# A four-mixer scan block on one core: a head's token-major operands moved to the partitions of its feature-major ones

## The chip, the cores and the metric

The kernel runs on one core of one Trainium2 chip. A core has TensorE (PE: matrix products, with PEld for the loading of its stationary operand), VectorE (DVE), ScalarE (ACT), GpSimd (POOL) and SyncE (SP, which here issues nearly all DMAs). They run side by side, each through its own instructions in a fixed order, and wait for each other by semaphores. On-chip memory (SBUF, and PSUM for the results of TensorE) has 128 partitions; a product sums over the partitions of its two operands. The metric is the device time in microseconds.

## The reference

One layer of a trunk over 256 context and 2048 latent tokens of width 1024: a modulated RMS norm, one input projection whose columns feed four mixers, an output projection with a gated residual, a second norm, an MLP with squared ReLU, and a final norm. All in float32.

```python
def _gla_scan(q, k, v, log_a):
    ...
    att = jnp.einsum('bhnik,bhnjk->bhnij', q * jnp.exp(g - g_mid), k * jnp.exp(g_mid - g))
    att = jnp.where(_tri(0), att, 0.0)
    s_loc = jnp.einsum('bhnck,bhncv->bhnkv', k * jnp.exp(g_end[..., None, :] - g), v)
    def step(s, xs):
        s_l, ge = xs
        return jnp.exp(ge)[..., None] * s + s_l, s
    ...
    o = jnp.einsum('bhnik,bhnkv->bhniv', q * jnp.exp(g), s0) + jnp.einsum('bhnij,bhnjv->bhniv', att, v)
```

The other three mixers (mLSTM, RWKV-7 and Gated DeltaNet) have the same form with more terms: four heads each, chunks of 64 tokens, and an output that is a sum of two products, one with the state before the chunk (a sum over features) and one with the values of the chunk (a sum over its tokens). RWKV-7 and Gated DeltaNet also solve a triangular system in each chunk. Each mixer scans forward and backward, and the two results are added.

## The kernel before

The tokens are 36 chunks of 64. Six rounds (`ROUNDS`) of chunks pass through the input projection and leave every scan operand in device memory, in two layouts: feature-major (`x_fm`: 64 features of a head on 64 partitions, tokens along the row) and token-major (`x_tm`: 64 tokens on the partitions). `solve` inverts the triangular systems (`x_t`). Then come 72 calls of `group(d, c0)`, one for each direction and chunk, each for all four mixers and their 16 heads: two heads side by side in the row (`ft`), two on the two halves of the partitions (`par`). Eight of them (the context chunks) only update the state, 64 also give outputs. Where both directions have met, `finish` norms and gates the sum and stores it to `x_mix`. `tails` is the output projection and the MLP, on blocks of 512 tokens, with products of 128 x 128 by 512 columns.

`body` writes the program: the calls of `group` are strewn between the pieces of the rounds (32 calls), of the output gates (16) and of the first third of `tails` (24). A scheduler then settles the order on each engine from the dependences and its own estimate of durations, so that an edit in `group` moves instructions throughout. Tiles come from pools with a fixed number of buffers (two for most in the rounds and the tail, four in the gate phase); a transfer into a buffer waits until its earlier content was last read.

A call of `group` does the following. `ps_att` and `ps_ml` hold the products of the chunk's queries and keys; masks and decays make them the token-major operands. `ps_R` is the right side of the solve, made from the state; `ps_U` is the solution; `ps_S` the update of the state; the new state `St` is the old one by a decay (GpSimd) plus `ps_S` (VectorE). `ps_ym` and `ps_ylgr` are the outputs.

Before, a head's token-major operands lay on the other half of the partitions from its feature-major ones, in one tile: `L[:, par, x]` holds 64 rows of features and 64 rows of tokens, and `st[:, par, c]` the state beside the values of the tokens, which a DMA brings into the state's tile. One product over all 128 rows then gives the sum of both terms. The price is that each elementwise instruction that writes into `L` or `st` covers 64 partitions and stands twice, once for each `par`. `weave` orders the products of a bank and `mm` issues those without accumulation (both are one line for all callers, L228 and L239 in the profile; L184, L192 and L197 are the helpers `tt`, `stt` and `act`, and L200 is `dma`).

```python
        for par in R(2):
            q = other[par]
            self.tt(L[q, par, x], rk[q, x], m3[q, x], ALU.mult)
...
        self.weave(b, [(q, f2[ft], L[:, par, 1 + ft], st[:, par, cr(ft)]) for ft, par, p, q in fp]
                   + [(q, g2[ft], kw[p, ft], st[p, par, f2[ft]]) for ft, par, p, q in fp])
```

Of the kernel before, what the change touches and what calls it, by code (L numbers as in the profile page):

```python
# [96 lines left out]
def host_layout(I):  # L97
# [50 lines left out]
    A["nw"] = np.stack([f[k][0].reshape(2, 2, 64)[:, ::-1].transpose(0, 2, 1).reshape(128, 2)  # L148
# [5 lines left out]
    wo = f["w_out"][0].reshape(4, 2, 2, 64, 1024)[[0, 2, 3, 1]][:, :, ::-1].transpose(0, 2, 1, 3, 4).reshape(KT, 128, 1024)  # L154
# [21 lines left out]
class Kern:  # L176
# [133 lines left out]
    def scratch(self):  # L310
# [23 lines left out]
        self.td = 386, 1038  # L334
# [14 lines left out]
    def fill(self):  # L349
# [5 lines left out]
        for ft in range(2):  # L355
            c = 256 + 129 * ft
# [339 lines left out]
    def row_out(self, r, d, k0, t, p0):  # L696
# [3 lines left out]
        if k0 < 2:  # L700
            for par in range(2):
                self.dma(o[:, 1 - par, :, k0].rearrange("c f t -> f c t"), t[p0 + n * par:p0 + n * par + n, 0])
        else:
            self.dma(o[:, :, :, k0:k1].rearrange("c h f k t -> (h f) c (k t)"), t[p0:p0 + 2 * n].rearrange("p k t -> p (k t)"))
# [70 lines left out]
    def col_out(self, r, d, f0, srcs):  # L775
# [213 lines left out]
    def rw_group(self, r, ft, c0, c1, k, kk, wa, rr, v, gl):  # L989
# [68 lines left out]
        self.tm_out(r4(vt), X["tm"][c0:c1, :, :, 64 * ft:64 * ft + 64], nc_)  # L1058
# [21 lines left out]
    def ml_round(self, r):  # L1080
# [17 lines left out]
        yield from self.v_tiles(r, 18, 257)  # L1098
# [82 lines left out]
    def gl_round(self, r):  # L1181
# [54 lines left out]
        yield from self.v_tiles(r, 24, 128)  # L1236
# [95 lines left out]
    def solve_prep(self, d, c0, sN, A, B):  # L1332
# [18 lines left out]
        for par in R(2):  # L1351
            self.dma(gc[SL[par]].rearrange("p c k f -> p c (k f)"), X["tm"][c0:c0 + 2, :, 1 - par, self.td[d] + 320:self.td[d] + 326].rearrange("c t w -> t c w"))
# [23 lines left out]
    def solve_post(self, d, c0, sN, sD, sT, A, B):  # L1376
# [59 lines left out]
    def state_tile(self):  # L1436

        return self.wp.tile([128, 2, 514], F32, tag="St", name="St", bufs=4)
# [12 lines left out]
    def group(self, d, c0):  # L1451
# [5 lines left out]
        other = sl[::-1]  # L1457
# [12 lines left out]
        if hasq:  # L1470
            o = 13 if d else 6
            self.dma(kc, X["fm"][:, c0, o:o + 14])
        else:
            o = self.slot(d, 0)
            self.dma(ka[:, :4], X["fm"][:, c0, o:o + 4])
            self.dma(cfm[:, :2], X["fm"][:, c0, 13:15])
# [11 lines left out]
        tms, tmd = (tm[:, 0:320], tm[:, 320:652]) if d else (tm[:, 332:652], tm[:, 0:332])  # L1488
# [20 lines left out]
        for ft in R(2):  # L1509
            x, n = (2 * ft, 2) if hasq else (1 + ft, 1)  # L1510
            both = [(p, q, L[p, par]) for par, (p, q) in enumerate(zip(sl, other))]
            for p, q, l in both:
                self.mm(rk[q, x:x + n], ka[p, 3 * ft], l[:, x:x + n])
            if hasq:
                for p, q, l in both:
                    self.mm(ra[q, ft], ka[p, 1 + ft], l[:, 3 * ft])
                for p, q, l in both:
                    self.mm(pk[q, ft], cfm[p, ft], cfm[p, 2 + ft])
# [12 lines left out]
        if hasq:  # L1531
# [4 lines left out]
            for par in R(2):  # L1536
                q = other[par]
                self.tt(L[q, par, 6:8], ga[q], pk[q], ALU.mult)
        kw = self.wt("kw", [2, 64])
        self.tt(kw, cfm[:, 0:2], gr(2), ALU.mult)  # L1540
        if hasq:

            for par in R(2):
                p = sl[par]
                k2 = "p (k f) t -> p k f t"
                self.tt(L[p, par, 6:10].rearrange(k2, k=2), cfm[p, 2:6].rearrange(k2, k=2), rw[p, :, 3:5].rearrange("p f k t -> p k f t"),
                        ALU.mult)
# [5 lines left out]
        if hasq:  # L1553
# [26 lines left out]
            for par in R(2):  # L1580
                q = other[par]
                self.G.tensor_copy(L[q, par, 4:6], lS[q])
# [5 lines left out]
        fp = [(ft, par, sl[par], other[par]) for ft in R(2) for par in R(2)]  # L1588
# [339 lines left out]
```

## Time and profile before

| | us |
|---|---|
| median of 3 runs | 4356.84 (4348.51 to 4357.94) |
| the profiled execution | 4357.55 |
| its span | 4355.7 |
| busy in the span: TensorE | 3487.9 (80%) |
| VectorE | 2629.0 (60%) |
| GpSimd | 1557.1 (36%) |
| ScalarE | 1379.0 (32%) |

The span is what the profiler saw between the first and the last instruction. Busy time is the union of an engine's instructions. A row of the profile's groups names the line, the engine, the operation, the tile written and the tiles read, the tile shape of a product (rows*columns of the array) and partitions x elements; `ps_ylgr<-St,L 128*64 128x64` is a product into the bank `ps_ylgr` over 128 rows. Each of these products is two instructions on TensorE. A row of the waits names who waited for whom, the sum in us, how often, and the longest.

### The profile page before, as it was taken

The numbers are of one execution on the slowest core, as the hardware profiler recorded it, in microseconds if no ns is written. First come the engines' busy times: TensorE is split into PE (matmuls) and PEld (weight loads), VectorE is DVE, ScalarE is ACT, GpSimd is POOL, SyncE is SP. The second block draws the span as 40 slices with busy tenths as digits, with TensorE's granted clock in tenths as the row PEclk, the third lists the DMA queues.
The fourth block names the chain that finished last, engine by engine and source line by source line (L and its number), as shares of the span: only waits on it lengthen the run. The fifth ranks groups of instructions, "written<-read, shape, count | busy, mean of one in ns | idle before, by whom it ended". The sixth has DMA issues, their size and how long they took to land. (4 is left out here: it accounts for less than half of the span.)

```text
span 4355.7 us, 71098 instructions
## 1 busy us (share of the span) xinstructions
PE 3487.9 (80%) x26458; PEld 2787.2 (64%) x26458; DVE 2629.0 (60%) x5775; ACT 1379.0 (32%) x2482; POOL 1557.1 (36%) x1883
## 2 busy tenths in 40 slices
PE   6355876776686876655878699999999999999998
PEld 5234555555564655545766477777778878877886
DVE  7653765666386667636777466767774445445444
ACT  3224332432432233222323133222322332333322
POOL 3222635644154253512324333334542142224122
PEclk9667866886787687757778799999999999999999
DMA  6586466765766665577676544446453334332332
GB/s 213 123 181 153 101 161 153 162 127 141 149 161 124 166 155 129 129 176 169 176 196 181 160 129 145 137 151 167 134 155 100 96 100 131 97 97 87 116 94 86
DMA packets 718873, 610.62 MB, mean 140 GB/s; under 512 B 384784, under 2 KB 594784, under 8 KB 718528
## 3 DMA queue, kind: packets, MB, share of 16 engines
q1 hardware_dynamic: 718528, 606.08, 54.0%
q8 instruction: 209, 3.42, 0.4%
q14 instruction: 136, 1.11, 0.1%
HBM read 470.86 MB, written 135.03 MB: 139 GB/s over the span
## 5 line engine op out<-in xcount | busy, mean ns | idle before, releaser
L184 POOL TENSOR_TENSOR w_lo<-w_f,w_hi 128x1024 fp32r<-128x1024 f32 x213 | 518.3, 2433 | 1104.3 <-ACT w_hi L197 1074.0
L197 ACT ACTIVATE w_hi<-w_f 128x1024 fp32r<-128x1024 f32 (+1 forms) x427 | 448.3, 1050 | 935.4 <-PE ps_a L239 360.8
L239 PE MATMUL ps_a<-ah,w_hi 128*128 128x512 f32 x1024 | 406.4, 403 | 11.6 <-ACT ah L197 9.9
L239 PE MATMUL ps_f<-h2l,w_hi 128*128 128x512 f32 x1024 | 403.5, 394 | 9.3 <-DVE h2l L192 9.2
L239 PE MATMUL ps_f<-h2h,w_hi 128*128 128x512 f32 x1024 | 404.7, 396 | 4.0 <-ACT w_hi L197 2.7
L239 PE MATMUL ps_a<-al,w_hi 128*128 128x512 f32 x1024 | 405.0, 396 | 0.0
L239 PE MATMUL ps_f<-h2h,w_lo 128*128 128x512 f32 x1024 | 403.3, 394 | 1.0 <-DVE w_lo L184 1.0
L184 DVE TENSOR_TENSOR w_lo<-w_f,w_hi 128x1024 fp32r<-128x1024 f32 (+1 forms) x214 | 268.0, 1252 | 220.1 <-ACT w_hi L197 204.6
L239 PE MATMUL ps_a<-ah,w_lo 128*128 128x512 f32 x1024 | 397.7, 396 | 0.0
L239 PE MATMUL ps_z<-hh,w_hi 128*128 128x512 f32 (+3 forms) x760 | 308.7, 413 | 76.3 <-ACT hh L197 22.3
L192 DVE SCALAR_TENSOR_TENSOR x1T<-ps_a,modv,x1T 128x512 f32<-128x512 f32 x256 | 187.6, 747 | 227.7 <-PE ps_a L239 227.3
L239 PE MATMUL ps_z<-hh,w_lo 128*128 128x512 f32 (+3 forms) x760 | 307.1, 405 | 22.2 <-DVE w_lo L184 13.9
L239 PE MATMUL ps_z<-hl,w_hi 128*128 128x512 f32 (+3 forms) x760 | 304.6, 401 | 5.4 <-DVE hl L184 5.3
L184 DVE TENSOR_TENSOR relu<-relu 128x512 f32<-128x512 f32 x128 | 185.6, 1451 | 102.8 <-ACT relu L197 102.6
L211 PE MATMUL ps_z<-w_hi,hh 128*128 128x256 f32 x672 | 209.9, 314 | 38.0 <-ACT w_hi L197 17.2
L239 PEld LDWEIGHTS ps_a<-ah,w_hi 128*128 128x128 f32 x1024 | 192.0, 189 | 67.3 <-ACT ah L197 20.0
L239 PEld LDWEIGHTS ps_z<-hh,w_hi 128*128 128x128 f32 (+1 forms) x760 | 159.4, 211 | 116.8 <-ACT hh L197 24.6
L239 PEld LDWEIGHTS ps_f<-h2l,w_hi 128*128 128x128 f32 x1024 | 193.6, 189 | 51.7 <-DVE h2l L192 11.2
L239 PEld LDWEIGHTS ps_f<-h2h,w_hi 128*128 128x128 f32 x1024 | 194.0, 190 | 46.8 <-ACT w_hi L197 4.5
L239 PEld LDWEIGHTS ps_f<-h2h,w_lo 128*128 128x128 f32 x1024 | 193.8, 189 | 42.9 <-DVE w_lo L184 1.9
L239 PEld LDWEIGHTS ps_a<-ah,w_lo 128*128 128x128 f32 x1024 | 193.9, 189 | 42.6 <-issue 0.4
L239 PEld LDWEIGHTS ps_a<-al,w_hi 128*128 128x128 f32 x1024 | 193.8, 189 | 42.3 <-DVE al L184 0.4
(414 smaller groups left out, 8000.4 us busy)
## 6 DMA issues: line engine op xcount, KB each, us to landing
w_f<-w SPq DMA_DIRECT2D x256, 512.0 KB
w_f<-wg SPq DMA_DIRECT2D x90, 512.0 KB
kc<-x_fm SPq DMA_DIRECT2D x64, 448.0 KB
adaw<-ada SPq DMA_DIRECT2D x48, 512.0 KB
tm<-x_tm SPq DMA_DIRECT2D x144, 163.0 KB
rw<-x_rows SPq DMA_DIRECT2D x144, 160.0 KB
w_f<-wp SPq DMA_DIRECT2D x44, 512.0 KB
gat<-x_gat SPq DMA_DIRECT2D x64, 288.0 KB
```

What stands on the lines that cost most here:

```text
L184: return (e or self.V).tensor_tensor(out=o, in0=a, in1=b, op=op)
L192: return self.V.scalar_tensor_tensor(o, a, s, b, op0, op1)
L197: return self.S.activation(o, a, f, bias=bias, scale=scale)
L211: i = self.T.matmul(o, l, r, start=k == 0, stop=k == len(mms) - 1)
L239: return self.T.matmul(o, l, r, start=start, stop=stop)
```

## The change

Token-major operands move to the same half as the feature-major ones. So the tile `L` falls into three: `ff` (a part of the loaded tile `fm`), `Lq` and `Lt`; the values come into the tile `tm` and no longer into the state's; the state's tile is half as wide (514 columns for 2 x 514). An elementwise instruction covers 128 partitions and stands once. The two terms of a sum are now two products of 64 rows that accumulate in the bank. The second half of `ps_U` is no longer copied into the state's tile by VectorE (line 1602): ScalarE's copy `U` takes both halves. GpSimd's copy of `lS` into `L` (line 1582) is gone, since the product reads `lS`. The operands of one step lie together in `x_fm` and `x_tm`, so one DMA brings `fm` in place of three (`L` twice and `kc`), and the two for `tm` also bring what two for `St` did. Weights and norms are permuted on the host to suit, and the rows of `x_rows` are stored in one DMA for two.

```diff
-        return self.wp.tile([128, 2, 514], F32, tag="St", name="St", bufs=4)
+        return self.wp.tile([128, 514], F32, tag="St", name="St", bufs=4)
...
-        L = self.lt("L", [2, 10, 64])
-        lo, w = (0, 6) if hasq else (1, 2)
-        for par in R(2):
-            o = self.slot(d, 7 + lo)
-            self.dma(L[sl[par], par, lo:lo + w], X["fm"][sl[par], c0, o:o + w])
-        for par in R(2):
-            self.dma(st[other[par], par, 128:514], X["tm"][c0, :, 1 - par, 0:386])
-        kc = self.lt("kc", [14, 64])
-        ka, cfm = (kc[:, 7:14], kc[:, 0:7]) if d else (kc[:, 0:7], kc[:, 7:14])
+        fm = self.lt("fm", [20, 64])
+        ff, ka, cfm = (fm[:, x:x + n] for x, n in (((14, 6), (7, 7), (0, 7)) if d else ((0, 6), (6, 7), (13, 7))))
         if hasq:
-            o = 13 if d else 6
-            self.dma(kc, X["fm"][:, c0, o:o + 14])
+            o = 13 if d else 0
+            self.dma(fm, X["fm"][:, c0, o:o + 20])
...
-        tm = self.lt("tm", [652])
-        o = 718 if d else 386
-        self.by_half(tm, X["tm"][c0, :, :, o:o + 652])
+        tm = self.lt("tm", [1038])
+        o = 332 if d else 0
+        self.by_half(tm, X["tm"][c0, :, :, o:o + 1038])
...
-        for par in R(2):
-            q = other[par]
-            self.tt(L[q, par, x], rk[q, x], m3[q, x], ALU.mult)
+        self.tt(Lt[:, x], rk[:, x], m3[:, x], ALU.mult)
...
-            for par in R(2):
-                q = other[par]
-                self.G.tensor_copy(L[q, par, 4:6], lS[q])
...
-        self.weave(b, [(q, f2[ft], L[:, par, 1 + ft], st[:, par, cr(ft)]) for ft, par, p, q in fp]
-                   + [(q, g2[ft], kw[p, ft], st[p, par, f2[ft]]) for ft, par, p, q in fp])
+        self.weave(b, [(p, f2[ft], Lt[p, 1 + ft], vr(ft)[p]) for ft, p in fp]
+                   + [(p, f2[ft], ff[p, 1 + ft], st[p, cr(ft)]) for ft, p in fp]
+                   + [(p, g2[ft], kw[p, ft], st[p, f2[ft]]) for ft, p in fp])
...
-        U = self.wt("U", [128])
-        self.act(U, b.t[:, 0:128], AF.Copy)
-        for par in R(2):
-            q = other[par]
-            self.V.tensor_copy(st[q, par, 0:128], b.t[q, 128:256])
+        U = self.wt("U", [256])
+        self.act(U, b.t[:, 0:256], AF.Copy)
...
-        for par in R(2):
-            p = sl[par]
-            o = new[p, par, 0:256]
-            self.tt(o, o, b.t[p, 0:256], ALU.add)
...
+        self.tt(new[:, 0:256], new[:, 0:256], b.t[:, 0:256], ALU.add)
...
-                    first.append((q, y, L[:, par, x], st[:, par, c]))
+                    first.append((p, y, f[p], st[p, c]))
+                    then.append((p, y, t[p], v[p]))
                     if mm == "r":
-                        then.append((q, y, ara[q, ft], U[q, f2[ft]]))
-            self.weave(b, first + then)
+                        last.append((p, y, ara[p, ft], U[p, f2[ft]]))
+            self.weave(b, first + then + last)
```

What this does to the order of the instructions shows at three places, all in the part of the tail where the last steps still run. First TensorE, at the end of one step, between two products of the MLP (`ps_a`): what stood there before (`L` is the joined tile, `St` the joined state, `ara` an attention term; the shape is output rows x columns, x4 a repeat).

```order
L239 MATMUL ps_a<-ah,w_lo 128x512
L228 MATMUL ps_ylgr<-St,L 64x64
L228 MATMUL ps_S<-St,mke 32x65 x4
L228 MATMUL ps_S<-St,tm 32x64 x4
L228 MATMUL ps_S<-St,ke 64x64 x4
L228 MATMUL ps_S<-St,tm 64x64 x4
L228 MATMUL ps_S<-U,tm 64x64 x4
L228 MATMUL ps_ylgr<-St,L 64x64 x7
L228 MATMUL ps_ylgr<-U,ara 64x64 x4
L239 MATMUL ps_a<-ah,w_lo 128x512
```

And now, at the end of a step in the same part:

```order
L228 MATMUL ps_ylgr<-St,Lq 64x64 x2
L228 MATMUL ps_S<-tm,mke 32x65 x4
L228 MATMUL ps_S<-tm 32x64 x4
L228 MATMUL ps_S<-tm 64x64 x4
L228 MATMUL ps_S<-U,ke 64x64 x4
L228 MATMUL ps_S<-U,tm 64x64 x4
L228 MATMUL ps_ylgr<-St,Lq 64x64 x2
L228 MATMUL ps_ylgr<-St,fm 64x64 x4
L228 MATMUL ps_ylgr<-tm,glS_223 64x64 x4
L228 MATMUL ps_ylgr<-U,Lt 64x64 x4
L228 MATMUL ps_ylgr<-tm,Lt 64x64 x4
L228 MATMUL ps_ylgr<-U,ara 64x64 x4
```

`ps_S` has as many products as before; `ps_ylgr` has 28 for 16 in the whole step, and the change from products over 128 rows (`ps_ylgr<-St,L`) to products over 64 (`ps_ylgr<-U,ara`) within the bank is gone, as is that between `ps_S` and `ps_ylgr`.

Second VectorE, at the update of the state in that part; before (`fs` and `leg` are decays, `relu` and `al` belong to the MLP):

```order
L1602 COPY St<-ps_U 64x128 x2
L184 TENSOR_TENSOR relu<-relu 128x512
L184 TENSOR_TENSOR al<-relu,ah 128x512
L184 TENSOR_TENSOR St<-St,ps_S 64x256
L192 SCALAR_TENSOR_TENSOR St<-St,fs_82,ps_S 64x130
L192 SCALAR_TENSOR_TENSOR St<-St,leg,ps_S 64x128
L184 TENSOR_TENSOR St<-St,ps_S 64x256
L192 SCALAR_TENSOR_TENSOR St<-St,fs_82,ps_S 64x130
L192 SCALAR_TENSOR_TENSOR St<-St,leg,ps_S 64x128
L184 TENSOR_TENSOR L<-kc,rw 64x256 x2
```

And now:

```order
L184 TENSOR_TENSOR relu<-relu 128x512
L184 TENSOR_TENSOR al<-relu,ah 128x512 x2
L184 TENSOR_TENSOR St<-St,ps_S 128x256
L192 SCALAR_TENSOR_TENSOR St<-St,fs_82,ps_S 128x130
L192 SCALAR_TENSOR_TENSOR St<-St,leg,ps_S 128x128
L184 TENSOR_TENSOR yall<-ps_ylgr,gat 128x384
```

Ten instructions of the step became four; one of them, the product for `Lq`, stands ten rows behind the update now.

Third SyncE, the loads of one step among those of the MLP's weights (`w_f`); before (`t_26099` is the solved system's tile, `rw` the rows of gates, `gat` the gates and the other direction's output):

```order
L200 DMA L<-x_fm 64x384 x2
L200 DMA St<-x_tm 64x386 x2
L200 DMA rw<-x_rows_103 64x640 x2
L200 DMA w_f<-w 128x1024 x2
L200 DMA gat<-x_gat 64x1152 x2
L200 DMA w_f<-w 128x1024
L200 DMA x_mix<-sq 128x512
L200 DMA kc<-x_fm 128x896
L200 DMA t_26099<-x_t_132 128x2x128
L200 DMA w_f<-w 128x1024
L200 DMA tm<-x_tm 64x652
```

And now:

```order
L200 DMA fm<-x_fm 128x1280
L200 DMA tm<-x_tm 64x1038 x2
L200 DMA rw<-x_rows_103 64x640 x2
L200 DMA w_f<-w 128x1024
L200 DMA gat<-x_gat 64x1152 x2
L200 DMA w_f<-w 128x1024
L200 DMA x_mix<-sq 128x512
L200 DMA w_f<-w 128x1024
L200 DMA t_26538<-x_t_132 128x2x128
```

The loads of `kc` and of `tm`, which stood apart from those of `L` and `St`, now stand with `fm`, at the place where `L` stood.

More of the change, by code (lines that the diff above doesn't have):

```diff
@@ L699, in row_out @@
         o = self.X[f"rows{r}"][d]
[L700 to L704, printed above, removed]
+        self.dma(o[:, :, :, k0:k1].rearrange("c h f k t -> (h f) c (k t)"), t[p0:p0 + 2 * n].rearrange("p k t -> p (k t)"))
     def part(self, c):
@@ L1097, in ml_round @@
         yield
-        yield from self.v_tiles(r, 18, 257)
+        yield from self.v_tiles(r, 18, 589)
     def ml_scalars(self, r):
@@ L1235, in gl_round @@
             yield
-        yield from self.v_tiles(r, 24, 128)
+        yield from self.v_tiles(r, 24, 460)
     def common_pools(self):
@@ L1510, in group @@
             x, n = (2 * ft, 2) if hasq else (1 + ft, 1)
-            both = [(p, q, L[p, par]) for par, (p, q) in enumerate(zip(sl, other))]
-            for p, q, l in both:
-                self.mm(rk[q, x:x + n], ka[p, 3 * ft], l[:, x:x + n])
+            for p in sl:
+                self.mm(rk[p, x:x + n], ka[p, 3 * ft], ff[p, x:x + n])
             if hasq:
[L1515 to L1518, printed above, removed]
+                for p in sl:
+                    self.mm(ra[p, ft], ka[p, 1 + ft], ff[p, 3 * ft])
+                for p in sl:
+                    self.mm(pk[p, ft], cfm[p, ft], cfm[p, 2 + ft])
         m3 = self.rwm[d].rearrange("p (a t) -> p a t", t=64)
         x = slice(0, 4) if hasq else slice(1, 3)
-        for par in R(2):
-            q = other[par]
-            self.tt(L[q, par, x], rk[q, x], m3[q, x], ALU.mult)
+        self.tt(Lt[:, x], rk[:, x], m3[:, x], ALU.mult)
         if hasq:
@@ L1559, in group @@
             pm, ps = (b[:, x:x + 128].rearrange("p (f t) -> p f t", f=2) for x in (0, 128))
-            for par in R(2):
-                self.mm(pm[other[par]], cfm[sl[par], 6], cfm[sl[par], 4:6])
-            for par in R(2):
-                q = other[par]
-                self.tt(L[q, par, 8:10], md[q], pm[q], ALU.mult)
+            for p in sl:
+                self.mm(pm[p], cfm[p, 6], cfm[p, 4:6])
+            self.tt(Lt[:, 6:8], md, pm, ALU.mult)
             lS = self.glS[d][s % 2]
@@ L1587, in group @@
         b = chb("ps_R")
-        fp = [(ft, par, sl[par], other[par]) for ft in R(2) for par in R(2)]
-        self.weave(b, [(q, f2[ft], L[:, par, 1 + ft], st[:, par, cr(ft)]) for ft, par, p, q in fp]
-                   + [(q, g2[ft], kw[p, ft], st[p, par, f2[ft]]) for ft, par, p, q in fp])
+        fp = [(ft, p) for ft in R(2) for p in sl]
+        vr, vl, vm = (lambda ft, c=c: vs[:, c(ft).start - 128:c(ft).stop - 128] for c in (cr, cl, cm))
+        self.weave(b, [(p, f2[ft], Lt[p, 1 + ft], vr(ft)[p]) for ft, p in fp]
+                   + [(p, f2[ft], ff[p, 1 + ft], st[p, cr(ft)]) for ft, p in fp]
+                   + [(p, g2[ft], kw[p, ft], st[p, f2[ft]]) for ft, p in fp])
         rR, gR = self.wt("rR", [128]), self.wt("gR", [128])
@@ L1615, in group @@
         e = 0 if d else 63
[L1616 to L1628 removed]
+        for x, eg in ((0, rw[:, :, 3, e:e + 1]), (128, self.reg[:, d, :, c0:c0 + 1])):
+            y = slice(x, x + 128)
+            self.tt(v3(new[:, y]), v3(st[:, y]), eg.to_broadcast([128, 2, 64]), ALU.mult, e=self.G)
+        self.tt(new[:, 0:256], new[:, 0:256], b.t[:, 0:256], ALU.add)
+        for x, y, w, f in ((384, 256, 65, self.fs[d]), (256, 321, 64, self.leg[:, d])):
+            tw = lambda t: t.unsqueeze(1).to_broadcast([128, 2, w])
+            self.stt(new[:, x:x + 2 * w].rearrange(s3, f=2), tw(st[:, x:x + w]), f[:, c0:c0 + 1], tw(b.t[:, y:y + w]), ALU.mult, ALU.add)
         if not hasq:
@@ L1639, in group @@
             b = self.bank(self.qa, "yy", "ps_y" + ms, 1)
-            first, then = [], []
+            first, then, last = [], [], []
             for mi, mm in enumerate(ms):
                 w = 65 if mm == "m" else 64
-                for ft, par, p, q in fp:
+                for ft, p in fp:
                     y = slice(128 * mi + w * ft, 128 * mi + w * ft + w)
-                    x, c = {"m": (8 + ft, cm(ft)), "l": (4 + ft, cl(ft)), "g": (6 + ft, f2[ft]), "r": (3 * ft, cr(ft))}[mm]
-                    first.append((q, y, L[:, par, x], st[:, par, c]))
+                    f, c, t, v = {"m": (Lq[:, 2 + ft], cm(ft), Lt[:, 6 + ft], vm(ft)), "l": (ff[:, 4 + ft], cl(ft), lS[:, ft], vl(ft)),
+                                  "g": (Lq[:, ft], f2[ft], Lt[:, 4 + ft], U[:, g2[ft]]),
+                                  "r": (ff[:, 3 * ft], cr(ft), Lt[:, 3 * ft], vr(ft))}[mm]
+                    first.append((p, y, f[p], st[p, c]))
+                    then.append((p, y, t[p], v[p]))
                     if mm == "r":
-                        then.append((q, y, ara[q, ft], U[q, f2[ft]]))
-            self.weave(b, first + then)
+                        last.append((p, y, ara[p, ft], U[p, f2[ft]]))
+            self.weave(b, first + then + last)
             if ms == "m":
```

68 lines of the change are left out of this document (25 added, 43 removed).

## The prediction

> **What bounds the kernel now.** I read the busy times by stage first, then what TensorE waits for, then the products one by one, and last the groups of VectorE, GpSimd and SyncE. The stages are mine: the rounds and the gate phase (545 to 2440 us, where 48 of the 72 group steps end), the MLP tail while the other 24 still run (2440 to 3290), the tail alone. Columns: the stage, its length, then busy time with the number of instructions for TensorE, its weight loads, VectorE, ScalarE, GpSimd; granted TensorE clock, share of the DMA engines, GB/s.
>
> ```profile
> span 4355.7 us, 71098 instructions
> 545.00:2440.00 1895.00, 1343.47 (x14177) 1090.84 (x14176) 1218.34 (x3095) 619.70 (x1281) 747.73 (x1129) 0.73 0.65 154
> 2440.00:3290.00 850.00, 804.60 (x6218) 620.56 (x6219) 582.36 (x1318) 252.50 (x422) 342.34 (x337) 0.97 0.52 151
> 3290.00:4355.70 1065.70, 1027.35 (x4440) 829.28 (x4438) 495.18 (x530) 331.18 (x428) 285.02 (x136) 0.99 0.32 100
> ```
>
> The last stage holds no group step and stays as it is. In the one before it TensorE is busy 804.60 of 850 us: there the end moves with TensorE's own work. Before 2440 nothing is full: TensorE 71%, VectorE 64%. There the kernel lives on waits, and an instruction saved is worth what it shortens of one. These are TensorE's waits that the change touches (total, times, longest), first six before 2440, then two after:
>
> ```profile
> PE ps_R L228 <- DVE L L184: 40.0, 11, 11.9
> PE ps_att L239 <- DMA L<-x_fm: 18.5, 10, 5.1
> PE ps_S L228 <- DVE St L1602: 18.1, 11, 3.8
> PE ps_R L228 <- DVE St L192: 12.9, 5, 4.3
> PE ps_ym L228 <- DVE L L184: 11.7, 3, 6.9
> PE ps_ml L239 <- DVE L L184: 6.9, 11, 2.3
> ...
> PE ps_R L228 <- DVE L L184: 6.8, 2, 5.8
> PE ps_ym L228 <- DVE L L184: 3.0, 3, 2.3
> ```
>
> All the waits ahead of 2440 except the one on a DMA are for half-height VectorE work: 89.6 us in 41 waits, of 552 us that TensorE is idle there.
>
> **TensorE: more products, fewer changes of tile shape.** Counted in the code, a step with outputs has 20 products more (ps_R 8 to 12, ps_ym 4 to 8, ps_ylgr 16 to 28), one without has 4 more: 24 x 20 = 480 in the tail, 40 x 20 + 8 x 4 = 832 before it. Their price stands in one stretch of the tail; first column the start:
>
> ```profile
> 2810.35 0.45 PE L228 MATMUL ps_S<-St,ke 64*64 64x64 f32 x8
> 2810.63 0.40 PE L228 MATMUL ps_S<-St,tm 64*64 64x64 f32 x8
> 2810.86 0.40 PE L228 MATMUL ps_S<-U,tm 64*64 64x64 f32 x8
> 2811.20 0.92 PE L228 MATMUL ps_ylgr<-St,L 128*64 128x64 f32 x24
> 2812.04 0.45 PE L228 MATMUL ps_ylgr<-U,ara 64*64 64x64 f32 x8
> 2812.42 0.50 PE L239 MATMUL ps_a<-ah,w_hi 128*128 128x512 f32 x1
> ```
>
> A product of 64 columns is two instructions (12 products stand as x24). From start to start, 24 instructions of shape 128*64 take 0.84 us, 24 of shape 64*64 (ps_S) 0.85, eight of 64*64 0.38. So the 64-row product costs no less than the 128-row one: (0.84 - 0.38) / 16 = 0.029 us an instruction, 0.0575 a product, and each run of one shape carries 0.38 - 8 x 0.029 = 0.15 us beside. In the order of the instructions I counted the places where the tile shape changes: 492 before and 378 now in the tail, 1012 and 852 ahead of it. Tail: 480 x 0.0575 = 27.6 us more, 114 x 0.15 = 17.1 less, **+10.5**, with nothing to hide it on an engine 95% busy. Of it, 5 waits on L (9.8 us) shrink by about 0.8 us each, -4: **+6.5**.
>
> Ahead of the tail: 47.8 - 24 = 23.8 us at full clock, 32.6 at the granted 0.73. It ranges from nothing (all of it in the 552 idle us) to +32.6; since a group's products come in bursts that others wait for, I take half: **+16**.
>
> The Trainium skill speaks against the change here: "TensorEngine Tiling (Array Packing)", Restrictions and Gotchas, says that different row tiles cannot write one PSUM bank at the same time. The ps_S rows are two row tiles in one bank and run no slower than ps_ylgr's column tiles (0.85 against 0.84), so the trace doesn't bear it out; it is the last rival below.
>
> **VectorE and ScalarE: half as many half-height instructions.** The rows: instruction, partitions x elements, count; busy, mean ns; idle before.
>
> ```profile
> L184 DVE TENSOR_TENSOR L<-kc,rw 64x256 f32<-64x256 f32 x128 | 68.4, 534 | 23.7 <-DMA rw<-x_rows 11.9 <-issue 9.3 <-PE ps_ylgr L228 0.6
> L184 DVE TENSOR_TENSOR St<-St,ps_S 64x256 f32<-64x256 f32 x144 | 59.9, 416 | 30.9 <-PE ps_S L228 29.6
> L184 DVE TENSOR_TENSOR L<-ps_att,pack 64x256 f32<-64x256 f32 x128 | 54.0, 422 | 22.5 <-PE ps_att L239 19.2
> L192 DVE SCALAR_TENSOR_TENSOR St<-St,leg,ps_S 64x128 f32<-64x128 f32 x144 | 49.6, 344 | 0.1
> L192 DVE SCALAR_TENSOR_TENSOR St<-St,fs,ps_S 64x130 f32<-64x130 f32 x144 | 49.5, 343 | 0.0
> L1602 DVE COPY St<-ps_U 64x128 f32<-64x128 f32 x144 | 41.6, 289 | 23.3 <-ACT U L197 21.0
> L184 DVE TENSOR_TENSOR L<-md,ps_ml 64x128 f32<-64x128 f32 x128 | 36.5, 285 | 24.9 <-PE ps_ml L239 22.2
> L184 DVE TENSOR_TENSOR L<-ga,ps_att 64x128 f32<-64x128 f32 x128 | 36.5, 285 | 1.9
> L184 DVE TENSOR_TENSOR s_s_x<-s_s_b,ps_n 128x256 f32<-128x256 f32 x32 | 13.3, 415 | 12.2 <-ACT s_s_x L197 11.5
> ...
> L197 ACT ACTIVATE U<-ps_U 128x128 f32<-128x128 f32 x72 | 19.7, 274 | 84.8 <-PE ps_U L239 84.6
> L197 ACT ACTIVATE s_s_x<-ps_n 128x256 f32<-128x256 f32 x32 | 12.0, 374 | 31.1 <-PE ps_n L239 29.1 <-DMA s_s_x<-x_bg 1.9
> ```
>
> 128x256 takes 415 ns and 64x256 416 to 422: height is free. One of each pair goes, and both copies of line 1602: 534 + 416 + 422 + 344 + 343 + 285 + 285 + 2 x 289 = 3.2 us a step with outputs, about 2.1 us (416 + 344 + 343 + 578, and a shorter mask) without. Ahead of the tail 40 x 3.2 + 8 x 2.1 = 145 of VectorE's 1218 us. What shows of it at the end: ps_R's 11 waits for L lose a mask half and an Lq half (0.95 each, 10.5), its 5 for St half an update (1.10, 5.5), ps_S's 11 both copies (0.58, 6.4), ps_ym and ps_ml's 14 one product (0.29, 4.0): 26.4 as the floor. The ceiling is the 89.6 us of these waits. I take **-35**, near the floor, with a little for waits on VectorE in which the removed work only stands in the queue. ScalarE's U grows from 128 to 256 columns, 0.1 us as the two rows show, between ps_U and ps_S: 11 such waits, **+1**.
>
> **GpSimd** loses two copies and two of four multiplications a step:
>
> ```profile
> L184 POOL TENSOR_TENSOR St<-St,rw 64x128 f32<-64x128 f32 x144 | 71.4, 496 | 270.9 <-PE ps_ylgr L228 100.5 <-DMA rw<-x_rows 74.3 <-DVE St L184 27.8
> L1582 POOL COPY L<-glS 64x128 f32<-64x128 f32 x128 | 48.7, 381 | 233.5 <-DVE glS L1576 227.9 <-PE ps_z L239 1.7
> ```
>
> That is 2 x 0.38 + 2 x 0.50 = 1.8 us on an engine busy 748 of 1895, and a place where its queue stood for VectorE goes (233.5 us idle). TensorE's list has almost no wait for these: nothing, and 5 us at most.
>
> **SyncE: fewer and longer transfers.** Issue times on its queue, then its waits, then VectorE's largest wait for a load ahead of 2440:
>
> ```profile
> 2149.52 1.24 SPq L200 DMA_DIRECT2D St<-x_tm  x2
> 2156.39 1.09 SPq L200 DMA_DIRECT2D L<-x_fm  x2
> 2169.80 0.60 SPq L200 DMA_DIRECT2D kc<-x_fm  x1
> ...
> SPq L200 <- PE ps_ml L239: 82.3, 27, 11.8
> SPq L200 <- PE ps_S L228: 71.9, 24, 9.0
> SPq L200 <- PE ps_ylgr L228: 17.2, 14, 4.1
> ...
> DVE ga L184 <- DMA tm<-x_tm: 59.0, 16, 18.4
> ```
>
> L, St and kc (1.09 + 1.24 + 0.60) become one fm (0.60, as kc): 2.33 us a step, 108 us ahead of the tail with 1.8 for the steps without outputs, and 24 row stores of 0.6 less. Bytes stay. A load that is waited for can come 2.33 us sooner: 10 waits of ps_att (18.5 us) bound the gain on TensorE, 16 x 2.33 = 37 us that on VectorE, of which 35/145 reaches the end, 9. I take **-10** of the 27.5, since a wait that lies behind a weight load gains nothing. Against it stands a new lifetime: kc was free after ps_ml, tm after ps_S; fm and tm are both read until ps_ylgr. Behind the waiting issue stand all later transfers of SyncE, weights too. L had that lifetime already, so mostly the wait exists; from 0 to +59 (that row doubled), I take **+6**.
>
> Sum: 6.5 + 16 - 35 + 1 - 10 + 6 = -15.5 (rounded -16). The profiled execution took 4357.55 us (span 4355.7 and 1.9 around it), 0.7 above the median of the three runs. **4341.5 us.**
>
> **The rivals.**
> *TensorE decides ahead of the tail too* (slower): its added work comes whole, +32.6, and VectorE's saving stays at 26.4, loads gain nothing, tail +10.5: 4375. It decides once the group's bursts meet ready weights behind them, which the 0.71 busy share and the 804.60 us of the tail speak for; the 41 waits speak against it.
> *The longer lifetimes decide* (slower): if fm and tm come late for the steps of the rounds, whose tiles have two buffers, as often again as tm does now, +59 in place of -10 + 6, less what VectorE's slack takes (half): about 4375 to 4400. For it: 154 us of SyncE's waits end at ps_ml and ps_S, earlier points than ps_ylgr. Against: L came that late already.
> *The waits go whole* (faster by more): -89.6 for -35, -27.5 for -10: about 4270 to 4300. For it: 145 us off VectorE and 122 off SyncE; against it: another wait stands right behind most.
> *It cancels*: the terms are small against 4357 and of both signs: 4349 to 4366.
> *Row tiles take turns at a bank*: the 48 products of ps_R, ps_ym and ps_ylgr of a step would cost 0.0575 more each, 66 us in the tail and 110 ahead of it: about 4515. Against it: ps_S, as above. This is the mechanism that the section of the Trainium skill named above states.
> That the change doesn't do what it says is out: the order shows 20456 products for 19144 and 5105 VectorE instructions for 5729.
>
> **How the numbers follow.** The forecast (4310 to 4349) 0.42, the large gain 0.10, cancelled 0.20, TensorE 0.14, lifetimes 0.12, row tiles 0.02. Within 0.2% means within 8.7 us, about what a measurement of this kernel can tell from no change. Faster 0.52, same 0.20, slower 0.28. The range runs into both slower rivals and most of the large gain: 4288 to 4398; the faster cases alone would be 4288 to 4349.
>
> **What would show it.** Right: the tail between its first and last group step 5 to 12 us longer with TensorE's mean clock unchanged; ps_R's wait for Lt and St down by a third; no VectorE wait for U's copies; VectorE about 220 us less busy in all, TensorE's 64*64 runs of 24 still near 0.85. Wrong: a tail shorter than before, SyncE waiting for ps_ylgr by more than the 154 us that it waited for ps_ml and ps_S, VectorE waiting longer for tm, or a start-to-start time of 64*64 products above 0.035 us at full clock. The order of instructions moves as a whole with the change, and this sum knows only the group steps: an unlucky order in a round would make it wrong by itself.

## The result, and the profile after

The changed kernel takes 4427.09 us (median of 4 runs, 4420.90 to 4428.57) against 4357.39 for the kernel before (4 runs, 4348.51 to 4362.67): **1.0159 of the time before, 95% interval 1.0140 to 1.0179**. It is 1.6% slower.

First the busy times by stage, columns as in the prediction; the second stage begins here with the first product of the output projection, `ps_o`.

```profile
545.00:2463.60 1918.60, 1372.84 (x15894) 1143.75 (x15892) 1085.56 (x2696) 630.19 (x1291) 675.52 (x954) 0.76 0.64 154
2463.60:3360.00 896.40, 831.47 (x7173) 648.68 (x7174) 507.78 (x1101) 252.65 (x420) 303.59 (x243) 0.96 0.47 140
3360.00:4426.60 1066.60, 1028.50 (x4445) 830.16 (x4443) 496.79 (x531) 331.87 (x429) 285.40 (x136) 0.99 0.30 100
```

VectorE has lost what it was to lose: 2629.0 us busy before, 2423.5 now. The MLP alone is as long as it was. To place the loss, I take one mark that every kernel has, the first `ps_o`, and call all behind it the tail. The row of the tail of the kernel before, then of the changed one:

```profile
2448.10:4355.70 1907.60, 1831.95 (x10656) 1449.84 (x10656) 1077.52 (x1847) 582.90 (x849) 627.36 (x473) 0.98 0.40 122
```
```profile
2463.60:4426.60 1963.00, 1859.97 (x11616) 1478.85 (x11616) 1004.57 (x1631) 584.52 (x849) 588.99 (x378) 0.97 0.38 119
```

The tail is **55.4 us longer**: TensorE is busy 28.0 us more (960 instructions more, the 480 products) and idle 27.4 us more (103.0 for 75.7). Only 15.5 us of the loss lie ahead of the mark (2463.6 for 2448.1).

The price of the products is as predicted. TensorE in the tail of the changed kernel (start, us, operation):

```profile
2741.75 0.45 PE L239 MATMUL ps_U<-rR,t 64*64 64x64 f32 x8
2742.03 0.40 PE L239 MATMUL ps_U<-gR,t 64*64 64x64 f32 x8
2742.27 0.40 PE L228 MATMUL ps_ylgr<-St,fm 64*64 64x64 f32 x8
2742.50 0.40 PE L228 MATMUL ps_ylgr<-St,Lq 64*64 64x64 f32 x8
2742.73 0.40 PE L228 MATMUL ps_ylgr<-St,fm 64*64 64x64 f32 x8
2742.97 0.40 PE L228 MATMUL ps_ylgr<-tm,glS 64*64 64x64 f32 x8
2743.30 0.50 PE L239 MATMUL ps_a<-ah,w_lo 128*128 128x512 f32 x1
```

From start to start eight instructions take 0.23 us, 0.029 each, and the 48 with their change of shape 1.55, where 48 x 0.029 + 0.15 gives 1.54. The price of taking turns at the bank, 0.0575 us more a product, is not there: that rival is out.

The waits tell more. TensorE's ahead of the tail (545 to 2455 us), then TensorE's, VectorE's and SyncE's in the part of the tail with steps (2463.6 to 3360), all of the changed kernel:

```profile
PE ps_U L239 <- DVE gR L184: 45.1, 14, 11.6
...
PE ps_att L239 <- DMA fm<-x_fm: 42.7, 12, 8.9
PE ps_R L228 <- DVE Lt L184: 36.6, 11, 10.4
...
PE ps_ml L239 <- DVE Lt L184: 31.0, 16, 5.2
```
```profile
PE ps_yT L247 <- POOL yall L184: 28.4, 21, 4.5
```
```profile
DVE kw L184 <- DMA fm<-x_fm: 49.1, 19, 6.1
...
DVE ga L184 <- DMA tm<-x_tm: 26.0, 17, 3.7
```
```profile
SPq L200 <- DVE md L184: 121.6, 22, 9.8
SPq L200 <- PE ps_ylgr L228: 70.9, 29, 6.4
```

In the kernel before, the same stretch of the tail (2448.1 to 3290) had these three rows (one each of TensorE, VectorE and SyncE):

```profile
PE ps_yT L247 <- POOL yall L184: 8.7, 9, 1.7
```
```profile
DVE kw L184 <- DMA kc<-x_fm: 20.2, 16, 2.9
```
```profile
SPq L200 <- DVE md L184: 52.7, 20, 6.7
```

TensorE's wait for L and St at `ps_R` (40.0 + 12.9 us, now 36.6 for Lt) is down by a third and the wait for the copies of line 1602 is gone. Others have grown in their place: `ps_ml` waits 31.0 us for Lt where it waited 6.9 for L, `ps_U` 45.1 for VectorE where it waited 31.0, and `ps_att` 42.7 for the load `fm` where it waited 18.5 for `L`. In the tail VectorE waits more than twice as long for its first load, TensorE three times as long at `ps_yT`, and SyncE stands 70.9 us for `ps_ylgr` (4.8 before, beside 51.4 for `ps_ml` and 45.3 for `ps_S`, which end sooner in a step). One place in the timeline of the changed kernel shows what hangs on that. TensorE, at the end of a step; SyncE; VectorE; TensorE again (in brackets the idle time before, and its end):

```profile
2816.28 0.40 PE L228 MATMUL ps_ylgr<-St,fm 64*64 64x64 f32 x8
...
2816.97 0.40 PE L228 MATMUL ps_ylgr<-tm,Lt 64*64 64x64 f32 x8
```
```profile
2816.72 0.33 SPq L200 DMA_DIRECT2D fm<-x_fm  x1
2817.21 0.36 SPq L200 DMA_DIRECT2D w_f<-w  x1
2817.68 1.09 SPq L200 DMA_DIRECT2D tm<-x_tm  x2
2825.66 1.08 SPq L200 DMA_DIRECT2D rw<-x_rows  x2
```
```profile
2818.57 0.29 DVE L192 SCALAR_TENSOR_TENSOR yall<-s,yall 128x128 f32<-128x128 f32 x1
2820.77 0.29 DVE L184 TENSOR_TENSOR kw<-fm,rw 128x128 f32<-128x128 f32 x1 [1.91 <-DMA fm<-x_fm]
2820.98 0.42 DVE L184 TENSOR_TENSOR Lq<-fm,rw 128x256 f32<-128x256 f32 x1
2821.32 0.68 DVE L1663 TENSOR_REDUCE ss<-sq 128x8 f32<-128x512 f32 x1
...
2824.56 0.29 DVE L184 TENSOR_TENSOR ga<-rw,tm 128x128 f32<-128x128 f32 x1 [2.15 <-DMA tm<-x_tm]
...
2826.38 0.69 DVE L184 TENSOR_TENSOR yall<-yall,rs 128x512 f32<-128x512 f32 x1
```
```profile
2829.12 0.55 PE L247 MATMUL ps_yT<-pack,yall 128*128 128x128 f32 x3 [0.48 <-POOL yall L184]
```

The load of `fm` is issued 0.04 us after the last product with `fm` in `ps_ylgr` ends (2816.28 + 0.40), that of `tm` 0.3 us after the last with `tm` (2816.97 + 0.40). VectorE's queue holds the `kw` and `ga` that read these loads, of a later step, between the pieces of `finish` for the step just done. Both stand for their loads (1.91 and 2.15 us), and behind them stands the norm of `yall`, for which TensorE waits at `ps_yT`. SyncE's own queue is held up too: the load of `rw` waits until `md` (2825.30 us on VectorE, just behind `ga`) has read the earlier content of its buffer, and the loads behind it wait with it.

In the kernel before, at the place shown in the prediction where `ps_ylgr` starts at 2811.20, `kc` was issued 7.0 us ahead of that start, and `kw` did not wait:

```profile
2804.20 0.33 SPq L200 DMA_DIRECT2D kc<-x_fm  x1
```
```profile
2807.58 0.28 DVE L184 TENSOR_TENSOR kw<-kc,rw 128x128 f32<-128x128 f32 x1
```

### The profile page after: what moved, and what is told of

Its sections match the earlier page's. It is cut to its first block, busy times and chain, and to the rows that moved or that the text cites. A ratio compares the mean times of both kernels' runs of the same rounds, so it can differ in the third digit from the quotient of the medians.

```text
span 4426.6 us, 74802 instructions
## 1 busy us (share of the span) xinstructions
PE 3543.9 (80%) x29082; PEld 2868.2 (65%) x29082; DVE 2423.5 (55%) x5151; ACT 1389.9 (31%) x2482; POOL 1446.1 (33%) x1611
## 5 line engine op out<-in xcount | busy, mean ns | idle before, releaser
L239 PE MATMUL ps_z<-hh,w_hi 128*128 128x512 f32 (+2 forms) x760 | 310.2, 413 | 30.8 <-ACT hh L197 12.0
L239 PE MATMUL ps_z<-hh,w_lo 128*128 128x512 f32 (+2 forms) x760 | 309.0, 408 | 17.9 <-POOL w_lo L184 9.5
L239 PE MATMUL ps_z<-hl,w_hi 128*128 128x512 f32 (+2 forms) x760 | 306.7, 404 | 8.6 <-DVE hl L184 8.6
L184 DVE TENSOR_TENSOR relu<-relu 128x512 f32<-128x512 f32 x128 | 200.1, 1565 | 114.8 <-ACT relu L197 114.7
L239 PEld LDWEIGHTS ps_a<-ah,w_lo 128*128 128x128 f32 x1024 | 194.8, 190 | 45.1 <-DVE w_lo L184 2.1
L211 PE MATMUL ps_z<-w_lo,hh 128*128 128x256 f32 x672 | 208.1, 311 | 9.6 <-POOL w_lo L184 8.9
```

What stands on the lines that cost most here:

```text
L184: return (e or self.V).tensor_tensor(out=o, in0=a, in1=b, op=op)
L211: i = self.T.matmul(o, l, r, start=k == 0, stop=k == len(mms) - 1)
L239: return self.T.matmul(o, l, r, start=start, stop=stop)
```

## The experiments

Two theories. **P**: the added products cost their price everywhere. Its opposite in the expectations is W: they cost it only in the tail (28 us), and the rest of the loss is new waits. **L** says which waits: `fm` and `tm`, now read until `ps_ylgr` in two buffers, come too late, and VectorE's queue carries that to `ps_yT`. c_after is the changed kernel again; the others are edits of `group`, of the layout that it loads, of the number of buffers or (e19_ff3order) of `body`. In the table, "tail" is the span less the start of the first `ps_o`, and its difference from 1907.6. "Ahead" is that start against the kernel before on the same chip; since that was profiled on the first chip only, its mark is an estimate elsewhere: its median less 1909.5 (the tail of 1907.6, and 1.9 around the span). Tail and mark are read in one execution of a kernel, and the ratio from all: that execution was 16.2 us under the median for e17_s3fewer, 12.8 under for e3_halves, 9.3 for e12_fmcut and 7.5 for e15_ff3tm3, 9.8 over it for e2_fewer, and within 4 for the others. The kernel before took 4309 to 4357 us on the chips used.

| kernel | ratio to before, 95% | tail | ahead |
|---|---|---|---|
| changed | 1.0159 (1.0140 to 1.0179) | 1963.0, +55.4 | +16 |
| c_after | 1.0139 (1.0114 to 1.0164) | 1959.3, +51.7 | +4 |
| e1_added | 1.0091 (1.0065 to 1.0117) | 1929.3, +21.7 | +24 |
| e2_fewer | 0.9960 (0.9946 to 0.9975) | 1911.8, +4.2 | -14 |
| e3_halves | 1.0221 (1.0192 to 1.0250) | 1958.8, +51.2 | +33 |
| e4_fm3 | 1.0060 (1.0038 to 1.0082) | 1931.3, +23.7 | +5 |
| e6_split2 | 1.0055 (1.0038 to 1.0072) | 1936.7, +29.1 | -4 |
| e7_split3 | 0.9956 (0.9942 to 0.9970) | 1929.4, +21.8 | -43 |
| e9_order | 1.0118 (1.0096 to 1.0141) | 1945.4, +37.8 | +11 |
| e10_s3halves | 1.0161 (1.0135 to 1.0186) | 1954.0, +46.4 | +25 |
| e11_tm3 | 0.9959 (0.9942 to 0.9976) | 1902.8, -4.8 | -10 |
| e12_fmcut | 1.0019 (1.0003 to 1.0035) | 1920.4, +12.8 | -15 |
| e13_tmcut | 1.0089 (1.0059 to 1.0118) | 1942.9, +35.3 | +8 |
| e14_ff3 | 1.0140 (1.0118 to 1.0162) | 1931.6, +24.0 | +39 |
| e15_ff3tm3 | 1.0008 (0.9994 to 1.0021) | 1905.4, -2.2 | -1 |
| e16_Sthalves | 1.0102 (1.0077 to 1.0128) | 1941.7, +34.1 | +16 |
| e17_s3fewer | 0.9946 (0.9927 to 0.9964) | 1901.0, -6.6 | -33 |
| e18_best | 0.9956 (0.9939 to 0.9973) | 1915.2, +7.6 | -31 |
| e19_ff3order | 1.0123 (1.0106 to 1.0140) | 1929.4, +21.8 | +28 |

**The products alone.** To the kernel before:

```diff
+                   + [(q, slice(256, 320), kw[p, ft], st[p, par, f2[ft]]) for ft, par, p, q in fp])
...
+            if ms == "m":
+                extra = [(q, slice(256, 320), kw[p, ft], st[p, par, f2[ft]]) for ft, par, p, q in fp]
+            else:
+                extra = 3 * [(q, slice(384, 448), ara[q, ft], U[q, f2[ft]]) for ft, par, p, q in fp]
+            self.weave(b, first + then + extra)
```

> The kernel before, with as many 64*64 products as the change adds (20 in a step with outputs, 4 in one without), written to unused columns of the banks of ps_R, ps_ym and ps_ylgr, and never read. Theory P (the added products cost their whole price, ahead of the tail too): 27.6 us in the tail and 40 to 65 ahead of it, so 4425 to 4450. Theory W (products cost only in the tail; the rest of the loss comes from new waits): about 28 us, 4385.

42.5 us (4360.49 for 4317.98): between the two, nearer to W (28) than to P (68 at least). Its tail:

```profile
2432.60:4361.90 1929.30, 1868.82 (x11616) 1481.31 (x11616) 1077.16 (x1847) 582.28 (x849) 628.79 (x473) 0.98 0.38 120
```

TensorE is busy 36.9 us more, but idle 15.2 less: even here a part of the added work fills waits, and 21.7 remain. The number of products is that of the changed kernel, whose tail is 34 us longer still, although it has fewer changes of shape there: 379, by the order of the instructions in the traces, for 536 here and 493 in the kernel before. So products alone do not make its tail.

**Products taken out of the changed kernel**, and later (e17_s3fewer) out of e7_split3, the best one, which comes below:

```diff
-        self.weave(b, [(p, f2[ft], Lt[p, 1 + ft], vr(ft)[p]) for ft, p in fp]
-                   + [(p, f2[ft], ff[p, 1 + ft], st[p, cr(ft)]) for ft, p in fp]
+        self.weave(b, [(p, f2[ft], ff[p, 1 + ft], st[p, cr(ft)]) for ft, p in fp]
...
-                    then.append((p, y, t[p], v[p]))
+                    if mm == "m":
+                        then.append((p, y, t[p], v[p]))
```

> The changed kernel without 16 of the 20 added products of a step (in ps_R the product of Lt and tm, in ps_ylgr those of the second group are left out, so the output differs); all else stays. Theory P: 1088 products fewer, at 0.0575 to 0.079 us: 55 to 70 us faster than the changed kernel, 4355 to 4370. Theory W: the tail's part alone, 384 x 0.0575 = 22 us: about 4405.

> The best kernel so far without 16 of the 20 added products of a step (the same ones as in the other kernel with fewer products; the output differs). At the price that adding products showed, 42.5 us for 1312, 1088 fewer give 35 us: a ratio of about 0.9875. If products are worth the 80 us that leaving them out gave in the changed kernel: 0.977.

The first gave more than either theory allowed, about 80 us. But it also ends the life of `tm` earlier, takes `Lt` and `tm` out of `ps_R`'s wait, and so mixes P with L. In the second, where `tm`'s life is already cut, the tail is 28.4 us shorter than in e7_split3 (384 products, 22.1 at the price of the prediction), but the intervals of the two ratios overlap: the gain of the tail does not show in the whole, and neither expectation was met.

**VectorE's halves.** In the changed kernel (for Lq, the two other products of Lt, the scalings and updates of St in the same way):

```diff
-        self.tt(Lt[:, x], rk[:, x], m3[:, x], ALU.mult)
+        for p in sl:
+            self.tt(Lt[p, x], rk[p, x], m3[p, x], ALU.mult)
```

> The changed kernel with its 128-high operations on VectorE and GpSimd made again as two 64-high ones (Lt three times, Lq, the three updates of St, the two scalings): about 2.6 us of VectorE and 1 us of GpSimd more in each step, TensorE's work and the loads unchanged. If the shorter VectorE chain reached the end, as the prediction held (-35 ahead of the tail), this is 20 to 35 us slower than the changed kernel: 4447 to 4462. If another wait stood behind, it stays within 9 us of 4427.

0.006 to 0.008 over the changed kernel, 27 to 35 us, none of it in the tail (1958.8 for 1959.3 and 1963.0). The gain on VectorE is real and lies ahead of the tail, as predicted.

**The life of the loads.** Three buffers for `fm`:

```diff
-TLB = {"gat": 1, "sq": 1}
+TLB = {"gat": 1, "sq": 1, "fm": 3}
...
-        self.car, = self.phase_pools(es, "r", {"yall": 1}, {"pp": 2, "pc": 1}, "car")
+        self.car, = self.phase_pools(es, "r", {"yall": 1, "fm": 3}, {"pp": 2, "pc": 1}, "car")
```

> The changed kernel with three buffers in place of two for the load fm, in the rounds and in the tail (four in the gate phase, as it is). If the longer life of fm decides (TensorE waits 42.7 us for it ahead of the tail, 18.5 for L before; VectorE 87.9 and 49.1), this is 15 to 40 us faster than the changed kernel: 4387 to 4412. If not, within 9 us of 4427, with SyncE's wait for ps_ylgr gone and the time kept.

0.008 to 0.010 faster, with the same work: L holds. But not as the last sentence had it: SyncE's wait for `ps_ylgr` stayed (83.2 us in the tail; by the order of SyncE's instructions 55.9 of them stand ahead of an issue of `fm`), and VectorE's wait in the tail moved from `fm` to `tm`, 26.0 us in the changed kernel, now:

```profile
DVE ga L184 <- DMA tm<-x_tm: 57.6, 23, 5.6
```

Then the loads cut where their lives end, both or one of them, with two buffers or three (c_after is for the comparison). The cut of `fm`; that of `tm` is alike, into `vs` (386 columns) and `tm` (652), with the columns of `x_tm` in their old order:

```diff
-        fm = self.lt("fm", [20, 64])
...
+        ff, kc = self.lt("ff", [6, 64]), self.lt("kc", [14, 64])
+        ka, cfm = (kc[:, 7:14], kc[:, 0:7]) if d else (kc[:, 0:7], kc[:, 7:14])
...
+            self.dma(ff, X["fm"][:, c0, o:o + 6])
+            self.dma(kc, X["fm"][:, c0, x:x + 14])
```

> The changed kernel as it is, again, on the chip on which the next three run, so that they have it beside them: 1.016 of the kernel before, as the first time; a ratio under 1.012 would say that the first one was partly its chip.

> The changed kernel with its two long loads cut where their lives end, two buffers each: fm into ff (6 rows, read until ps_ylgr) and kc (14 rows, read until ps_ml), tm into vs (386 columns, read until ps_ylgr) and tm (652 columns, read until ps_S). One issue on SyncE more for fm and two for tm in each step. If the long life of the large tiles is the cost, as three buffers for fm said (43 us), most of it comes back: 25 to 45 us under the changed kernel, less 3 x 0.6 us of SyncE a step in part: a ratio of 1.006 to 1.010. If it was the number of buffers alone (ff and vs still live until ps_ylgr in two): 1.014 or more.

> The same cut, with three buffers for ff and vs in the rounds and the tail. If what is left of the loss is the wait for tm behind the one for fm (57.6 us of VectorE in the tail with three buffers for fm), both go: the price of the added products less VectorE's saving remains, 42 - 27: a ratio of 0.999 to 1.004. If more buffers for loads do nothing beyond those for fm: 1.006.

> The changed kernel with fm alone cut, into ff and kc, two buffers each; tm stays whole. If fm's life is the cost and tm's is not: as with both cut, a ratio of about 1.0055. If tm's life is: 1.014.

> The changed kernel with tm alone cut, into vs and tm, two buffers each; fm stays whole. If fm's life is the cost: 1.012 or more, as the changed kernel; if tm's is: 1.0055; if each holds a half: both single cuts near 1.010.

c_after's 1.0139 is over the 1.012 of its expectation. The two short lives with the same two buffers bring back 0.008 (e6_split2): it is the life, not the number of buffers alone. Of the single cuts, `fm`'s brings back more (1.0019) than `tm`'s (1.0089), and alone it does better than both together, which no theory had. e7_split3 is **faster than both kernels of the case** (0.9956), by more than the expectation.

More room for tm: e11_tm3 is e7_split3 with a third buffer for `tm` (and one in place of two for `mke`), e14_ff3 and e15_ff3tm3 are e12_fmcut with a third for `ff`, and for the whole `tm` too (below the last of them; the rounds have the same entries):

```diff
-TLB = {"gat": 1, "sq": 1}
+TLB = {"gat": 1, "sq": 1, "ff": 3, "tm": 3}
```

> The same kernel with the cut loads, with three buffers for tm too (and one in place of two for mke, to make room). VectorE waits 61.6 us for tm ahead of the tail and 42.3 in it. If that is again a wait that reaches the end: 10 to 25 us under the kernel with three for ff and vs, a ratio of 0.990 to 0.993. If other engines' waits stand behind it: 0.9956 as there.

> The changed kernel with fm cut into ff and kc, three buffers for ff in the rounds and the tail, tm whole with two. If ff's third buffer makes the gain of the best kernel (0.9956): 0.994 to 0.998. If it is the cut and the third buffer of vs: about 1.002, as with fm cut and two buffers.

> The same with three buffers for the whole tm too. If the lives of both loads count, with room for each: 0.988 to 0.995, under the best kernel, since it issues two transfers a step less on SyncE. If tm's life counts for little: as e14_ff3.

The tail answers: with three buffers for `tm` it is 1902.8 and 1905.4 us, under the kernel before in spite of the 480 products (1915.2 in e18_best, below, a little over it). The tail of e15_ff3tm3, and TensorE's wait for `yall` in it:

```profile
2427.60:4333.00 1905.40, 1845.18 (x11616) 1465.24 (x11616) 1025.74 (x1631) 586.65 (x849) 580.94 (x378) 0.99 0.39 121
```
```profile
PE ps_yT L247 <- POOL yall L184: 2.6, 3, 1.2
```

With the loads in time the wait at `ps_yT` falls from 28.4 to 2.6 us, TensorE's idle time from 103.0 to 60.2, and its busy time is 13.2 us over the kernel before where it was 28.0: the other 14.8 went as the mean granted clock rose (0.97 there, 0.99 here). SyncE's wait for `md`, 121.6 us in the changed kernel's tail, is 8.1 here and 2.6 in e11_tm3. Over the kernels the wait at `ps_yT` falls roughly as the tail does: 28.4 and 27.1 us in the changed kernel and c_after, 11.4 to 23.0 where a load is cut or `fm` has three buffers (e4, e6, e7, e12, e13, e14), 1.3 to 6.5 where `tm` has three (e11, e15, e18). The part ahead of the tail does not answer so. e11_tm3's tail gained 26.6 us on e7_split3's, and its ratio nothing; e14_ff3 met neither expectation, with +39 ahead of the tail against -15 for e12_fmcut, which has one buffer less; e15_ff3tm3 lies between its two.

One comparison was not run: the kernel before with more buffers. It too waits for its loads in the tail (VectorE 20.2 us for `kc` and 20.8 for `tm`, TensorE 8.7 at `ps_yT`), so how much of these gains it would share, and whether the change is worth anything beside them, is open.

**The order.** In the changed kernel, `t64` loaded ahead of `rw`; in e7_split3, a third buffer for `tm` in the tail alone; in e14_ff3, the steps of the second round begun sooner:

```diff
+        X64 = self.lt("t64", [2, 2, 64])
+        i = X["t64"][d, c0 // 2].rearrange("p (m c w) -> p m c w", m=2, c=2)
+        self.dma(X64.rearrange("p m f t -> p m (f t)"), i[:, :, c0 % 2])
         rw = self.lt("rw", [2, 5, 64])
```
```diff
-TLB = {"gat": 1, "sq": 1, "ff": 3, "vs": 3}
+TLB = {"gat": 1, "sq": 1, "ff": 3, "vs": 3, "tm": 3}
```
```diff
-            interleave(K.round_(1, r1), q, groups(F, [0, 1, 2, 3]) + groups(B, [3, 2, 1, 0, 35, 34]), 29, 0.3)
+            interleave(K.round_(1, r1), q, groups(F, [0, 1, 2, 3]) + groups(B, [3, 2, 1, 0, 35, 34]), 29, 0.25)
```

> The changed kernel with one load of a step (t64) issued ahead of the load rw in place of behind it: nothing is saved or added, but the scheduler sets the order of all engines anew. It measures what another order alone does: within 0.004 of the changed kernel's ratio if order is worth little; 0.01 or more would say that no single run here carries a conclusion of that size.

> The kernel with both loads cut and three buffers for ff and vs, with a third buffer for tm in the tail alone; its instructions stand in the same order as there up to the tail. If the tail's gain from tm's third buffer (1903 us from the first ps_o to the end, for 1929) stands by itself: a ratio of 0.988 to 0.991, with the time ahead of the tail as there, some 40 us under the kernel before. If the fast rounds there were chance of one run: 0.995 to 0.998.

> The kernel with fm cut and three buffers for ff (ratio 1.014), with the steps of the second round begun a little sooner (0.25 of the round for 0.3): the same work, in another order from the second round on. If its slow rounds (39 us over the kernel before, where two buffers for ff were 15 under it) come of the order: a ratio of 1.000 to 1.009. If a third buffer for ff is harmful by itself: 1.012 to 1.016.

e9_order left TensorE's order as it was up to the tail, so it says nothing of the rounds; in the tail it moved 14 us, so a difference of that size between two tails can be order alone. e18_best gained 14.2 us in the tail, half of what was expected, and nothing in the ratio. It has e7_split3's order ahead of the tail, and there the two stand at -43 and -31, the changed kernel's two runs at +16 and +4: about 12 us is what this estimate is good for between chips. e19_ff3order stayed slow (1.0123), so its order was not the whole cause. What e14_ff3 and e19_ff3order share is a late `tm` ahead of the tail (111.6 us of VectorE in the second); VectorE's wait for it in e14_ff3, then in e15_ff3tm3:

```profile
DVE ga L184 <- DMA tm<-x_tm: 139.3, 31, 16.7
```
```profile
DVE ga L184 <- DMA tm<-x_tm: 68.4, 20, 6.9
```

That would fit L (a sooner `ff` behind which `tm` still has two buffers). But e12_fmcut, with the same two buffers, waits 105.6 us for `tm` there and has no such loss, so the loss stays open.

**Halves again, where the loads are in time** (edits as above, all of them, then the update of St and its scalings alone):

> The kernel with the cut loads and three buffers for ff and vs, with every 128-high operation of a step on VectorE and GpSimd made again as two 64-high ones. In the changed kernel the same edit cost 0.006 to 0.008 of the time. If the late loads hid a part of what VectorE saves, the edit now costs more, 35 us or over: a ratio of 1.004 or more. If VectorE's saving is worth 27 us whatever the loads do: about 1.002.

> The best kernel so far (both loads cut, three buffers for ff and vs) with only the update of the state made in halves: three operations on VectorE more (1.1 us) and two on GpSimd (1.0 us) in each step, all behind ps_S, between one step and the next of its direction. If the 88 us of all halves sit in this chain: a ratio of 1.008 to 1.016. If they sit in the factors ahead of ps_R and the outputs: under 1.002.

All halves now cost 0.0205 of the time, some 88 us, 25 of them in the tail, and the update alone 0.0146, 12 in the tail, both as expected. Undoing VectorE's saving thus costs 2.5 to 3.3 times what it costs in the changed kernel, and in the tail 25 us where it cost none: that fits late loads that hid a part of it. How much of the 88 us is the order ahead of the tail, where these two stand at +25 and +16 against -43, is not settled.

## Why the prediction was wrong, step by step

**Right.** VectorE's busy time (205 us less, 220 named), the end of the copies, `ps_R`'s wait down by a third, the price of a 64-row product. The tail's +10.5 us for products less shape changes: once the loads are in time, TensorE is busy 13.2 us more there (e15_ff3tm3; 17.8 and 19.3 in e11_tm3 and e18_best), and the rows in the result section are the predicted price. The floor of VectorE's saving, 26.4 us, against 27 to 35 measured by undoing it (that run does not bring back the copies of line 1602).

**Wrong: the tail's +6.5.** It measured +55.4, and this is 49 of the 86 us by which the sum missed. The step that failed is the one on SyncE: "L had that lifetime already, so mostly the wait exists". It was priced ahead of the tail only, at +6. But a late `L` held up TensorE's `ps_att`; what VectorE does first in a step, `kw` and `ga`, read `kc` and `tm`, whose buffers were free at `ps_ml` and `ps_S`. Now these hang on `ps_ylgr` of an earlier step, and behind them in VectorE's queue stands `finish`. The prediction named a queue behind SyncE's wait, and none behind VectorE's. Giving the loads room took the whole loss of the tail away (e11_tm3, e15_ff3tm3; all but 7.6 us in e18_best), with all the added products kept. The rival "the longer lifetimes decide" had the mechanism, but placed it in the rounds, gave it 4375 to 4400, and took 154 us of SyncE's waits as the sign; SyncE waited 70.9 us for `ps_ylgr` in the tail and 46.5 ahead of it, under that sign: a wait of the queue's own says little where what it holds back is wanted at once. Another of the prediction's signs of being wrong, VectorE waiting longer for `tm`, pointed at the wrong load: ahead of the tail that wait went from 59.0 to 45.6 us, and `kw`'s, 27.3 us for `kc`, became 87.9 for `fm`.

**Wrong: the clock "unchanged".** Of the 28.0 us more that TensorE is busy in the tail, 14.8 are gone in e15_ff3tm3, where its waits are (0.97, then 0.99). The Trainium skill, "TensorE: Matmul & The Clock Gate", Part 1: The HAM clock gate, says that the array's clock follows how busy it has lately been; these two rows agree with it (103.0 us idle at 0.97, 60.2 at 0.99). A price of idle time cannot be read from the runs: e12_fmcut and e6_split2 are both idle for 77.8 us of their tails, both at 0.98, and busy for 1842.6 and 1858.9.

**Mis-sized: ahead of the tail, -22, measured +15.5.** Products: the +16 is what is left after the shape changes saved; e1_added, which adds the products and saves none, stands at +24, so this term was not shown to be too small. VectorE: -35 predicted; undoing it costs 27 to 35 us by the medians, and 17 to 29 by the profiled executions ahead of the tail, of which e3_halves' was the fast one named above. So the term that was mis-sized is the rest, the loads and `U`: -3 in the sum, and by these numbers +8.5 at the least and up to +26.5 (15.5 - 24 + 17 to 35), more if the products cost less than 24. TensorE's wait for the load at `ps_att`, 24.2 us longer there, speaks for the loads. Closer than that the terms cannot be told apart: twelve kernels with the same arithmetic in `group`, differing in buffers, cuts and order of their loads, spread from -43 to +39 us there, and why is open.

## What to carry to other kernels

Before merging loads, write for each row when its first and last reader run: the merged tile is free at the latest of the last ones and wanted at the earliest of the first, and with two buffers its load starts only when the step two before has ended. Follow a late load into the queue of the engine that reads it first, to what stands behind it there. If a merge is wanted all the same, cut it by life or give it a third buffer: here each alone took back more than half of the loss (e6_split2, e4_fm3), and both together turned 1.4 to 1.6% slower into 0.4% faster (e7_split3, e18_best). It is no rule without a measurement: e14_ff3, with both for `fm` alone, took back nothing of the time (1.0140).

## What the runs showed of the hardware that was not expected

The same program took 4427.1 us the first time and 4365.1 in c_after, and the kernel before beside them 4357.4 and 4309.1. That the chip makes the difference is likely, not shown for the first pair, whose chip is not on record: over two sets of runs on one chip the kernel before took 4340.6 and 4342.8 us, on three others 4309.1, 4318.0 and 4338.5. The tail of the changed kernel hardly takes part in it (1963.0 and 1959.3 us); its first `ps_o` starts at 2463.6 us in the one and 2403.3 in the other. So stretches ahead of the tail are compared across chips only through the kernel before.
